# Two transformer blocks on one core: the last layer's expert weights in runs of four rows a partition, and token rows modulated before they are gathered

## The chip, the cores and the metric

The kernel runs on one core of one Trainium2 chip. The core has a matrix engine (TensorE, PE in the profile), a vector engine (VectorE, DVE), a scalar engine (ScalarE, ACT), a GpSimd engine (POOL) and a sync engine (SyncE, SP) that only issues transfers; 16 DMA engines move data between DRAM and the on-chip memory of 128 partitions (SBUF). The metric is the device time of one execution in microseconds; the time of a kernel is the median of its runs.

## What is computed

All in float32, on 512 latent and 256 context tokens of width 1024. A first block of two layers, then a second block of one layer. In each layer of the first block an attention and convolution mixer comes first and then a mixture of experts in which each expert chooses its tokens. The change touches the experts alone:

```python
def modulate(h, shift, scale):
    return h * (1 + scale) + shift

def expert_choice_ffn(h, w_router, w_g, w_u, w_d):
    B, n, D = h.shape
    cap = CAPACITY_FACTOR * n // N_EXPERTS          # 64 latent, 32 context tokens
    logits = jnp.einsum('bnd,de->ben', h, w_router)
    aff = jax.nn.softmax(logits, axis=1)
    gate, idx = lax.top_k(aff, cap)
    xs = h[bi, idx]
    a = jnp.einsum('becd,edf->becf', xs, w_g)
    u = jnp.einsum('becd,edf->becf', xs, w_u)
    y = jnp.einsum('becf,efd->becd', jax.nn.silu(a) * u, w_d)
    return jnp.zeros_like(h).at[bi, idx].add(y * gate[..., None])

# in a layer, after the mixer:
h2 = modulate(rmsnorm(x, g_ffn[l]), sh2, sc2)
x = x + gt2 * expert_choice_ffn(h2, w_router[l], w_e_gate[l], w_e_up[l], w_e_down[l])
```

There are 16 experts a layer, each with three 1024 x 1024 weight matrices (`w_e_gate`, `w_e_up`, `w_e_down`), so that a layer reads 201 MB of expert weights. In the first layer the latent and the context tokens both go through the experts, in the last layer the latent ones alone.

## The kernel before

Stages, in order: mixer of layer 0 for the latent tokens (to about 635 us), the same for the context tokens (to about 873), experts of layer 0 for both (to about 1436), mixer of layer 1 (to about 2053), experts of layer 1 (`experts_local`, to about 2530), second block.

**Weights of the experts.** They pass through a ring of slots, each 128 partitions x 4 rows x 1024 floats (2 MB); a slot holds half of a matrix. `ring_load` (L884) fills one with two transfers of 1 MB on SP's queue; SP issues a load when the slot's last reader on PE is done, so the loads run ahead of their use by the length of the ring (10 slots in layer 0, 9 in layer 1). The source is viewed as `"(k p) f -> p k f"`: partition p gets rows p, 128+p, 256+p, 384+p of the half, and each row is a run of 4 KB on its own. A layer has 96 loads, 192 transfers.

**Token rows.** At the end of a mixer `project` makes the output product, adds it to the rows `xt` (tiles of 128 tokens), and for each tile computes the norm, the router's logits and a row tile `xn`, which is `xt` times the reciprocal norm r:

```python
xo = p.tile([128, D], FP32, name="xn", bufs=2)
self.scale(xo, xt[t], r, t)          # DVE for even tiles, ACT for odd ones (L358, L360)
nc.gpsimd.dma_start(self.dr[f"xn{st.name}{l}"][t * 128:t * 128 + 128], xo)   # L1082
```

There are two buffers for `xn`, and the stores stand in POOL's queue. `choose` then finds the tokens of each expert. `fetch` (L1216, POOL's queue) gathers the 128 chosen rows of two latent experts, or four context ones, from DRAM by an indirect transfer into `xg`. `gather` turns them: eight 128 x 128 transposes on PE (L141) into PSUM, and then eight copies of 128 x 128 to `xT`, each of which also applies the modulation, scale G and shift S being one value a partition there (`affine`: DVE L1127 and ACT L1125 in turn).

**An expert.** `up` (L1239) makes the gate and the up product from `xT` and four slots, `act` the activation `th`, `act_turn` turns it with four (latent) or two (context) transposes and copies it to `hT`, and `down_ps` (L1269) makes the down product from two slots. Matmuls take their operands in order on PE: what stands behind an instruction that waits, waits too. The kernel is built by Tile, a scheduler that puts each engine's instructions in an order at build time.

**The start of the experts of layer 0.** `expert0` fetches, turns and computes the latent part of expert 0 while the context mixer ends; everything else of the stage follows it on PE.

Of the kernel before, what the change touches and what calls it, by code (L numbers as in the profile page):

```python
# [8 lines left out]
FP32 = mybir.dt.float32  # L9
# [3 lines left out]
ACTF = mybir.ActivationFunctionType  # L13
ALU = mybir.AluOpType
# [4 lines left out]
D = 1024  # L19
# [18 lines left out]
class Kernel:  # L38
# [832 lines left out]

    def ring_load(self):

        e, r = divmod(self.nload, 6)
        which, k = divmod(r, 2)
        q, nm = self.cyc[self.nload % self.nring]
        self.nload += 1
        t = self.slots.pop(nm, None)
        if t is None:
            t = q.tile([128, 4, D], FP32, name=nm)  # L880
        src = self.A[("w_e_gate", "w_e_up", "w_e_down")[which]][self.rl, e, k * 512:(k + 1) * 512]
        src = src.rearrange("(k p) f -> p k f", p=128)
        for j in range(2):
            self.nc.sync.dma_start(t[:, 2 * j:2 * j + 2], src[:, 2 * j:2 * j + 2])  # L884
        self.rt[which, e, k] = t
# [149 lines left out]
    def project(self, l, st, wp, p, mg, src, dst, ring, extra):  # L1035

        nc, n, nt, A = self.nc, st.n, st.nt, self.A  # L1040
        gt = p.tile([128, D], FP32, name="gt1")
        md = self.dr[f"mod{l}"]
        nc.sync.dma_start(gt, md[st.s:st.s + 1, 2 * D:3 * D].to_broadcast([128, D]))
        xt = self.load_x(nc.sync, p if dst else self.xs, src, nt)
        wr = p.tile([128, KT, NE], FP32, name="wr")
        nc.sync.dma_start(wr, A["w_router"][l].rearrange("(k p) e -> p k e", p=128))
        ss = self.small.tile([128, 4, 4], FP32, name="ssp")
        G, S = st.aff2
        z = self.small.tile([128, 4, NE], FP32, name="rz", bufs=2)[:, :nt]
        gw = p.tile([128, KT, NE], FP32, name="gw")  # L1050
        sw = self.small.tile([128, NE], FP32, name="sw", bufs=1)

        def router(hs, ws):
            lg = self.s_ps(NE)
            for kt in range(KT):
                nc.tensor.matmul(lg, hs[:, kt], ws[:, kt], start=kt == 0, stop=kt == KT - 1)
            return lg

        def shift():

            sb = p.tile([128, KT, 128], FP32, name="h2", bufs=2)
            for kt in range(KT):
                nc.vector.tensor_copy(sb[:, kt], S[kt].to_broadcast([128, 128]))
                nc.vector.tensor_scalar(gw[:, kt], wr[:, kt], G[:, kt:kt + 1], None, op0=ALU.mult)
            nc.scalar.activation(sw, router(sb, wr), ACTF.Copy)

        def rows(t):

            s1 = self.small.tile([128, 1], FP32, name="s1")
            nc.vector.reduce_sum(s1, ss[:, t], axis=AX.X)  # L1070
            r, _ = self.rsqrt(s1, [128, 1], 1.0 / D, EPS)
            h = p.tile([128, KT, 128], FP32, name="h2", bufs=2)
            for q in range(2):
                tp = self.t_ps(128, 512)
                for i in range(4):
                    self.transpose(tp[:, i * 128:(i + 1) * 128], xt[t][:, (4 * q + i) * 128:(4 * q + i + 1) * 128])
                self.copy(h[:, 4 * q:4 * q + 4], tp.rearrange("p (k c) -> p k c", c=128))
            yield
            nc.vector.scalar_tensor_tensor(z[:, t % 2 * 2 + t // 2 if nt == 4 else t], in0=router(h, gw), scalar=r, in1=sw, op0=ALU.mult, op1=ALU.add)
            xo = p.tile([128, D], FP32, name="xn", bufs=2)  # L1080
            self.scale(xo, xt[t], r, t)
            nc.gpsimd.dma_start(self.dr[f"xn{st.name}{l}"][t * 128:t * 128 + 128], xo)  # L1082
            if not dst:
                self.kept.append(xt[t])
            yield

        tails = []
        for c in range(4):
            cs = slice(c * 256, c * 256 + 256)
            w = self.wblock(wp, A["w_out"][l, :, cs])  # L1090
            if ring and self.nload < len(self.cyc):
                self.ring_load()
            for t in range(nt):
                ts = slice(t * 128, t * 128 + 128)
                ps = self.mm_ps(128, 256)
                self.mm3(ps, mg, w, ts, slice(0, 256))
                y = p.tile([128, 256], FP32, name="py", bufs=2)
                nc.vector.tensor_mul(y, ps, gt[:, cs])
                nc.vector.tensor_add(xt[t][:, cs], xt[t][:, cs], y)
                if dst:  # L1100
                    nc.gpsimd.dma_start(self.dr[dst][ts, cs], xt[t][:, cs])
                nc.scalar.activation(y, xt[t][:, cs], ACTF.Square, accum_out=ss[:, t, c:c + 1])
                if c == 1 and t == 0:
                    shift()
                for g in tails:
                    next(g, None)
                if t % 2:
                    next(extra, None)
                if c == 3:
                    tails.append(rows(t))  # L1110
        for g in [*tails, extra]:
            self.drive(g)
        rm = self.small.tile([128, 2, 4], FP32, name="rmx")
        nc.vector.reduce_max(rm[:, 0, :nt], z, axis=AX.X)
        nc.vector.tensor_tensor(z, z, rm[:, 0, :nt, None].to_broadcast([128, nt, NE]), op=ALU.subtract)
        zf = z.rearrange("p t e -> p (t e)")
        self.exp(p, zf, zf, nt * NE)
        nc.vector.reduce_sum(rm[:, 1, :nt], z, axis=AX.X)
        nc.vector.reciprocal(rm[:, 1, :nt], rm[:, 1, :nt])
        nc.vector.tensor_tensor(z, z, rm[:, 1, :nt, None].to_broadcast([128, nt, NE]), op=ALU.mult)  # L1120
        return z
# [91 lines left out]
    def fetch(self, st, g, p):  # L1213
# [3 lines left out]
            out=st.xg, out_offset=None, in_=self.dr[f"xn{st.name}{st.l}"],  # L1217
            in_offset=bass.IndirectOffsetOnAxis(ap=st.gi[:, g:g + 1], axis=0))

    def gather(self, st, p, p_x, bufs=1):  # L1220

        nc, xg = self.nc, st.xg
        xT = p.tile([128, KT, 128], FP32, name="xT" + st.name, bufs=bufs)
        G, S = st.aff2
        for q in range(2):
            tp = p_x()
            self.pe_run([self.transpose(tp[:, i * 128:(i + 1) * 128], xg[:, (4 * q + i) * 128:(4 * q + i + 1) * 128])
                         for i in range(4)])
            for i in range(4):
                kt = 4 * q + i  # L1230
                self.affine(xT[:, kt], tp[:, i * 128:(i + 1) * 128], G[:, kt:kt + 1], S[kt], i)
        return xT

    def up(self, st, w, e, p_a):
# [20 lines left out]
    def act_turn(self, st, t, p, p_x):  # L1255

        nj = st.w // 128
        tp = p_x()[:, :nj * 128]
        self.pe_run([self.transpose(tp[:, j * 128:(j + 1) * 128], t[:, j * 128:(j + 1) * 128]) for j in range(nj)])
        hT = p.tile([128, 512], FP32, name="hT")[:, :nj * 128]  # L1260
        self.copy(hT, tp)
        return hT
# [158 lines left out]
    def block2(self):  # L1421
# [4 lines left out]
        with ExitStack() as es:  # L1426
# [164 lines left out]
            for t in range(nt):  # L1591
                nc.sync.dma_start(xs[t], self.dr["x2"][t * 128:(t + 1) * 128])
            out_b = project(1, xs, False)
            fill = [(q_gen(Qs, QA + 256, "q_norm_a_2", self.sk[:, 2, 4:8], 1), 5), (gates(Gs[3], GA, 1), 2)], [(out_b, 16)]
            for kv in range(2):
                Vh = [V_[:, t, kv * 64:kv * 64 + 64] for t in range(4)]
                self.section(attend(Qs.pop(0), [(kh[:, kv], kl[:, kv])] * 4, [Vh] * 4, 0, 2 * kv, Gs[2 + kv]),
                             fill[kv], last=kv == 1)
            self.drive(project(0, xs, True))


# [57 lines left out]
```

## Time and profile before

| | before |
|---|---|
| median of 3 runs | 2824.26 us (2823.77 to 2829.33) |
| profiled execution | 2827.67 us, of which the profile's span is 2825.9 us |
| mean granted clock of TensorE | 0.976 |
| PE, DVE, ACT, POOL busy | 93%, 49%, 34%, 4% of the span |
| DMA, mean over the span | 225 GB/s |

A busy share is a mean over stages that have different limits. The page also cuts the span into 40 equal slices, gives busy shares and DMA rates for each, and follows back the chain of work that ended last; windows, waits and timelines of single stretches come from the trace.

### The profile page before, as it was taken

The page shows a single profiled execution, that of the slowest core. Times are in us where ns is not written, and L with a number is a line of the kernel's source. Part 1 is how long each engine was busy: PE and PEld are TensorE (multiplying, and loading weights), DVE is VectorE, ACT ScalarE, POOL GpSimd, SP SyncE. Part 2 cuts the span into 40 slices and gives each one's busy share as a digit, 9 for nine tenths or more (in the row PEclk, how much of TensorE's full clock was granted, in tenths as well). Part 3 has the DMA queues.
Part 4 walks back from the last instruction along what each step waited for, and adds up shares of the span by engine and source line. Part 5 has one row for each costly group of instructions (what it writes and reads, how often), then busy time and mean ns, then how long its engine had stood idle before and what let it go on. Part 6 is the DMA issues. An engine that isn't in the chain of part 4 may idle for free. (4 is left out here: it accounts for less than half of the span.)

```text
span 2825.9 us, 43871 instructions
## 1 busy us (share of the span) xinstructions
PE 2635.3 (93%) x17509; PEld 1811.8 (64%) x17509; DVE 1382.9 (49%) x3755; ACT 962.8 (34%) x1966; POOL 117.6 (4%) x143
## 2 busy tenths in 40 slices
PE   7999999999998999999989999999789888879999
PEld 3788887789995455544437888878733222229878
DVE  4766676459764111111137665764622222238886
ACT  4445455225551000000034454553211000125763
POOL 0100000020001011111000000000000000000000
PEclk9999999999998999999989999999899999999999
DMA  8411211678466999999965212114789999983221
GB/s 291 161 61 60 75 49 59 229 267 299 150 215 223 379 374 384 391 391 387 386 233 171 67 55 75 51 61 131 297 351 409 409 409 409 409 337 87 61 90 60
DMA packets 273839, 635.96 MB, mean 225 GB/s; under 512 B 23924, under 2 KB 148292, under 8 KB 273636
## 3 DMA queue, kind: packets, MB, share of 16 engines
q1 hardware_dynamic: 258868, 595.31, 57.0%
q0 software_dynamic: 13744, 34.68, 4.0%
q8 instruction: 138, 2.26, 0.3%
q10 hardware_dynamic: 1024, 3.18, 0.3%
q14 instruction: 65, 0.53, 0.1%
HBM read 610.75 MB, written 22.35 MB: 224 GB/s over the span
## 5 line engine op out<-in xcount | busy, mean ns | idle before, releaser
L1239 PE MATMUL au<-we,xTlat 128*64 128x512 f32 x1984 | 451.3, 597 | 36.2 <-DMA we<-in_w_e_up_dram 23.4
L1239 PEld LDWEIGHTS au<-we,xTlat 128*64 128x64 f32 x1984 | 156.8, 137 | 320.0 <-issue 207.0
L219 PE MATMUL mm<-hhi,whi 128*128 128x512 f32 (+1 forms) x928 | 338.3, 365 | 0.0
L221 PE MATMUL mm<-hhi,wlo 128*128 128x512 f32 (+1 forms) x928 | 334.4, 360 | 0.0
L220 PE MATMUL mm<-hlo,whi 128*128 128x512 f32 (+1 forms) x928 | 332.6, 358 | 0.0
L199 DVE TENSOR_TENSOR wlo<-wraw,whi 128x1024 fp32r<-128x1024 f32 x234 | 285.6, 1222 | 92.7 <-ACT whi L198 90.8
L198 ACT ACTIVATE whi<-wraw 128x1024 fp32r<-128x1024 f32 x234 | 247.1, 1058 | 170.7 <-PE mm L220 93.6
L1269 PE MATMUL yp<-we,hT 128*32 128x256 f32 (+1 forms) x2016 | 286.6, 493 | 14.5 <-ACT hT L135 7.3
L219 PE MATMUL mm<-whi,hhi 128*128 128x256 f32 x736 | 218.0, 297 | 11.4 <-ACT qr L440 6.3
L1269 PEld LDWEIGHTS yp<-we,hT 128*32 128x32 f32 (+1 forms) x2016 | 112.1, 125 | 166.5 <-issue 109.5
L220 PE MATMUL mm<-wlo,hhi 128*128 128x256 f32 x736 | 214.0, 291 | 1.0 <-DVE wlo L199 1.0
L221 PE MATMUL mm<-whi,hlo 128*128 128x256 f32 x736 | 213.6, 292 | 0.0
L219 PEld LDWEIGHTS mm<-hhi,whi 128*128 128x128 f32 x928 | 175.8, 189 | 26.8 <-issue 4.9
L221 PEld LDWEIGHTS mm<-hhi,wlo 128*128 128x128 f32 x928 | 175.4, 189 | 25.5 <-issue 0.8
L220 PEld LDWEIGHTS mm<-hlo,whi 128*128 128x128 f32 x928 | 175.7, 189 | 24.1 <-issue 1.5
L582 ACT ACTIVATE PT<-tp 128x384 f32<-128x384 f32 (+2 forms) x392 | 142.5, 407 | 113.9 <-PE tp L141 111.6
L554 ACT ACTIVATE P<-S,mx,sc 128x768 f32<-128x768 f32 (+5 forms) x192 | 151.9, 792 | 80.1 <-DVE mx L551 73.2
L1250 ACT ACTIVATE th<-au 128x512 f32<-128x512 f32 (+1 forms) x47 | 24.6, 524 | 447.2 <-PE au L1239 447.2
L219 PEld LDWEIGHTS mm<-whi,hhi 128*128 128x128 f32 x736 | 144.9, 197 | 21.4 <-ACT qr L440 8.3
L1251 DVE SCALAR_TENSOR_TENSOR th<-th,au 128x512 f32<-128x512 f32 (+1 forms) x47 | 28.1, 597 | 247.3 <-ACT th L1250 247.3
L1252 DVE TENSOR_TENSOR th<-th,au 128x512 f32<-128x512 f32 (+1 forms) x47 | 28.1, 597 | 246.1 <-PE au L1239 246.1
L220 PEld LDWEIGHTS mm<-wlo,hhi 128*128 128x128 f32 x736 | 144.8, 197 | 4.3 <-issue 2.6
(319 smaller groups left out, 4560.4 us busy)
## 6 DMA issues: line engine op xcount, KB each, us to landing
we<-in_w_e_gate_dram SPq DMA_DIRECT2D x128, 1024.0 KB, 19.1
we<-in_w_e_up_dram SPq DMA_DIRECT2D x128, 1024.0 KB, 13.8
we<-in_w_e_down_dram SPq DMA_DIRECT2D x128, 1024.0 KB, 18.3
wraw<-in_w_in_dram SPq DMA_DIRECT2D x166, 512.0 KB, 3.8
wada<-in_w_ada_dram SPq DMA_DIRECT2D x96, 512.0 KB, 6.7
wraw<-in_w_branch_dram SPq DMA_DIRECT2D x36, 512.0 KB, 3.5
wraw<-in_w_out_dram SPq DMA_DIRECT2D x32, 512.0 KB, 3.6
xt<-in_x_dram SPq DMA_DIRECT2D x8, 512.0 KB, 8.0
```

Source lines behind the costliest of these rows:

```text
L198: self.nc.scalar.activation(hi, src, ACTF.Copy)
L199: self.nc.vector.tensor_sub(lo, src, hi.bitcast(FP32))
L219: nc.tensor.matmul(ps, lh, rh, start=k == 0, stop=False)
L220: nc.tensor.matmul(ps, lh, rl, start=False, stop=False)
L221: nc.tensor.matmul(ps, ll, rh, start=False, stop=k == n)
L554: nc.scalar.activation(P, S[:, c0:c1], ACTF.Exp, bias=mx[:, 1:2], scale=sc, accum_out=mx[:, 2:3])
L582: self.nc.scalar.activation(PT[:, s0:s0 + j - i, qc:qc + 128], tp[:, i * 128:j * 128].rearrange("p (s c) -> p s c", c=128), ACTF.Copy)
L1239: r = [self.nc.tensor.matmul(ps[j * st.cap:(j + 1) * st.cap], st.xT[:, kt, s0:s0 + st.cap], w[kt // 4][:, kt % 4, j * st.w:(j + 1) * st.w] ...
L1250: nc.scalar.activation(t, a, ACTF.Tanh, scale=0.5)
L1251: nc.vector.scalar_tensor_tensor(t, in0=t, scalar=1.0, in1=a, op0=ALU.add, op1=ALU.mult)
L1252: nc.vector.tensor_tensor(t, t, u, op=ALU.mult)
L1269: r = [self.nc.tensor.matmul(ps[o * st.cap:(o + 1) * st.cap], hT[:, j * 128 + q * st.cap:j * 128 + (q + 1) * st.cap], w[kt // 4][:, kt % 4 ...
```

## The change

Three edits go together.

1. In layer 1 a ring load views its source as `"(p k) f -> p k f"`: partition p gets rows 4p to 4p+3 of the half. The two transfers of a load then take two of these rows each, so a partition reads one run of 8 KB in each, at a distance of 16 KB from the next partition's. Layer 0 keeps its runs of 4 KB.
2. This permutes the rows over which the products of layer 1 contract. So the transposes in `gather` and `act_turn` take, in layer 1, every fourth column (`rows_of`): 8 for each of 8 gathers and 4 for each of 16 experts, 128 in all.
3. The modulation, whose values would be permuted too, moves from `gather` to `project`, in both layers. `row_mod` loads three rows broadcast to all partitions (scale, shift and the norm's gain, 512 KB each, on SP's queue) and makes the factor `gb` on DVE (128 x 1024). Each token tile (4 latent and 2 context ones in layer 0, 4 in layer 1) is scaled by r on ACT, then multiplied by `gb` and added to the shift on POOL, and then stored as before. `gather` now copies plainly, two copies of 128 x 512 (ACT L135 and DVE L137) in place of eight that modulate; there are 8 + 4 gathers in layer 0 and 8 in layer 1.

```diff
@@ ring_load
         src = self.A[("w_e_gate", "w_e_up", "w_e_down")[which]][self.rl, e, k * 512:(k + 1) * 512]
-        src = src.rearrange("(k p) f -> p k f", p=128)
+        src = src.rearrange("(p k) f -> p k f" if self.rl else "(k p) f -> p k f", p=128)
         for j in range(2):
             self.nc.sync.dma_start(t[:, 2 * j:2 * j + 2], src[:, 2 * j:2 * j + 2])
@@ project
         G, S = st.aff2
+        gb, sb2 = [p.tile([128, D], FP32, name=x) for x in ("gb", "sb")]
...
+        def row_mod():
+
+            gf = self.A["g_ffn"]
+            nc.sync.dma_start(gb, md[st.s:st.s + 1, 4 * D:5 * D].to_broadcast([128, D]))
+            nc.sync.dma_start(sb2, md[st.s:st.s + 1, 3 * D:4 * D].to_broadcast([128, D]))
+            g = p.tile([128, D], FP32, name="xn", bufs=2)
+            nc.sync.dma_start(g, gf[l:l + 1].to_broadcast([128, D]))
+            nc.vector.scalar_tensor_tensor(gb, in0=gb, scalar=1.0, in1=g, op0=ALU.add, op1=ALU.mult)
...
             xo = p.tile([128, D], FP32, name="xn", bufs=2)
-            self.scale(xo, xt[t], r, t)
+            nc.scalar.activation(xo, xt[t], ACTF.Copy, scale=r)
+            nc.gpsimd.tensor_mul(xo, xo, gb)
+            nc.gpsimd.tensor_add(xo, xo, sb2)
             nc.gpsimd.dma_start(self.dr[f"xn{st.name}{l}"][t * 128:t * 128 + 128], xo)
...
                 if c == 1 and t == 0:
                     shift()
+                    row_mod()
@@ gather, act_turn
+    def rows_of(self, st, x):
+
+        if st.l:
+            x = x.rearrange("t (c j) -> t j c", c=128)
+            return [x[:, j] for j in range(x.shape[1])]
+        return [x[:, j:j + 128] for j in range(0, x.shape[1], 128)]
...
-        G, S = st.aff2
         for q in range(2):
             tp = p_x()
-            self.pe_run([self.transpose(tp[:, i * 128:(i + 1) * 128], xg[:, (4 * q + i) * 128:(4 * q + i + 1) * 128])
-                         for i in range(4)])
-            for i in range(4):
-                kt = 4 * q + i
-                self.affine(xT[:, kt], tp[:, i * 128:(i + 1) * 128], G[:, kt:kt + 1], S[kt], i)
+            self.pe_run([self.transpose(tp[:, i * 128:(i + 1) * 128], x)
+                         for i, x in enumerate(self.rows_of(st, xg[:, 512 * q:512 * q + 512]))])
+            self.copy(xT[:, 4 * q:4 * q + 4], tp.rearrange("p (k c) -> p k c", c=128))
...
-        self.pe_run([self.transpose(tp[:, j * 128:(j + 1) * 128], t[:, j * 128:(j + 1) * 128]) for j in range(nj)])
+        self.pe_run([self.transpose(tp[:, j * 128:(j + 1) * 128], x) for j, x in enumerate(self.rows_of(st, t))])
```

The scheduler puts the new work into POOL's queue like this. Before, at the end of the context mixer of layer 0 (`Vctx` are the last loads of the context attention, the first `xglat` is the fetch for `expert0`, `c_64` are the mixer's output rows, `xnctx` the row tiles of the context, `x_63` the result of expert 0):

```order
L690 DMA Vctx_6179<-kcs_1120 128x256
L1216 DMA xglat<-xnlat_66,gilat_7458 128x1024
L1101 DMA c_64<-xt 128x256 x8
L1082 DMA xnctx_67<-xn 128x1024 x2
L1284 DMA x_63<-ylat,silat_7459 1024x512
L1216 DMA xglat<-xnlat_66,gilat_7458 128x1024
L1216 DMA xgctx<-xnctx_67,gictx_9484 128x1024
L1216 DMA xglat<-xnlat_66,gilat_7458 128x1024
L1216 DMA xgctx<-xnctx_67,gictx_9484 128x1024
L1284 DMA c_64<-yctx,sictx_9485 1024x256
L1216 DMA xglat<-xnlat_66,gilat_7458 128x1024
```

After, at the same place:

```order
L690 DMA Vctx_6191<-kcs_1114 128x256
L690 DMA Vctx_6194<-kcs_1120 128x256
L1116 DMA c_64<-xt 128x256 x8
L1095 TENSOR_TENSOR xn<-xn,gb 128x1024
L1096 TENSOR_TENSOR xn<-xn,sb 128x1024
L1095 TENSOR_TENSOR xn<-xn,gb 128x1024
L1097 DMA xnctx_67<-xn 128x1024
L1096 TENSOR_TENSOR xn<-xn,sb 128x1024
L1097 DMA xnctx_67<-xn 128x1024
L1232 DMA xglat<-xnlat_66,gilat_7473 128x1024
L1304 DMA x_63<-ylat,silat_7474 1024x512
L1232 DMA xglat<-xnlat_66,gilat_7473 128x1024
```

The first fetch stood ahead of the stores of the context rows; it now stands behind them, behind the four elementwise instructions of the two context tiles and behind their stores.

ACT's queue at the end of the mixer of layer 1, before (`h` are the turned rows for the router, `py` the squares for the norm, `xn` the scaled row tiles):

```order
L358 ACTIVATE xn<-xt,rsq 128x1024
L1102 ACTIVATE py,ssp<-xt 128x256
L135 ACTIVATE h_18469<-tp 128x512
L135 ACTIVATE h_18536<-tp 128x512
L1102 ACTIVATE py,ssp<-xt 128x256
L135 ACTIVATE h_18574<-tp 128x512
L358 ACTIVATE xn<-xt,rsq 128x1024
L1125 ACTIVATE xTlat<-tx,modT_144,G2lat_17873 128x128 x4
```

After, at the same place:

```order
L1094 ACTIVATE xn<-xt,rsq 128x1024
L1117 ACTIVATE py,ssp<-xt 128x256
L135 ACTIVATE h_18426<-tp 128x512
L1117 ACTIVATE py,ssp<-xt 128x256
L1094 ACTIVATE xn<-xt,rsq 128x1024 x2
L135 ACTIVATE h_18495<-tp 128x512
L1117 ACTIVATE py,ssp<-xt 128x256
L135 ACTIVATE h_18535<-tp 128x512
L1094 ACTIVATE xn<-xt,rsq 128x1024
L135 ACTIVATE xTlat<-tx 128x512
```

All four tiles are now scaled on ACT; the third of them (the second of the pair in one row) needs the buffer of the first, and stands ahead of the copies of `h` for the third and fourth tile.

## Rows read from the trace of the kernel before

**Rows 1.** The page: DMA rate in 40 slices, chain by line, a group.

```profile
GB/s 291 161 61 60 75 49 59 229 267 299 150 215 223 379 374 384 391 391 387 386 233 171 67 55 75 51 61 131 297 351 409 409 409 409 409 337 87 61 90 60
...
DMA we<-in_w_e_up_dram 7%; PE mm L219 4%; PE mm L221 3%; PE mm L220 3%; PE au L1239 3%; SPq L884 3%; PE yp L1269 2%; PE tp L141 2%; PE mm L630 1%; DVE wlo L199 1%; PE S L539 1%; PE yp L1383 1%; DVE xt L1387 0%; PE S L540 0%; DVE xq L483 0%
...
L199 DVE TENSOR_TENSOR wlo<-wraw,whi 128x1024 fp32r<-128x1024 f32 x234 | 285.6, 1222 | 92.7 <-ACT whi L198 90.8
```

**Rows 2.** Windows of both expert stages: busy us by engine, PEclk, DMA share, GB/s.

```profile
955.00:1440.00 485.00, 470.65 (x4273) 225.22 (x4268) 70.52 (x140) 37.77 (x78) 53.86 (x37) 1.00 0.98 371
...
2300.00:2400.00 100.00, 80.97 (x346) 27.47 (x344) 23.67 (x41) 9.38 (x18) 1.87 (x2) 0.95 1.03 409
```

**Rows 3.** DMA view, 2150 to 2500 us: packets; one queue (packets, MB, share).

```profile
DMA packets 37153, 143.23 MB, mean 409 GB/s; under 512 B 2219, under 2 KB 2219, under 8 KB 37141
...
q1 hardware_dynamic: 36421, 140.43, 100.5%
```

**Rows 4.** The same view, 1600 to 1900 us: packets and two queues.

```profile
DMA packets 17975, 18.13 MB, mean 60 GB/s; under 512 B 544, under 2 KB 17952, under 8 KB 17952
...
q1 hardware_dynamic: 17952, 17.83, 19.0%
q8 instruction: 14, 0.23, 0.3%
```

**Rows 5.** Line L884, 2064 to 2513 us: transfers, ns, first and last start.

```profile
L884 SPq DMA_DIRECT2D we<-in_w_e_down_dram x60: 367/2351/4417, 2068.1 to 2504.8; - x60
L884 SPq DMA_DIRECT2D we<-in_w_e_up_dram x58: 368/2406/4402, 2064.7 to 2494.1; - x58
L884 SPq DMA_DIRECT2D we<-in_w_e_gate_dram x56: 367/2348/4407, 2075.0 to 2484.3; - x56
```

**Rows 6.** Waits of PE, 2080 to 2512 us: us in total, times, longest.

```profile
PE au L1239 <- DMA we<-in_w_e_up_dram: 22.8, 38, 0.7
PE tx L141 <- ACT xTlat L1125: 15.3, 7, 2.3
```

**Rows 7.** Waits of PE, 955 to 1440 us.

```profile
PE tx L141 <- ACT xTlat L1125: 8.1, 6, 1.3
```

**Rows 8.** Timeline of POOL, 828 to 912 us: start us, us, instruction.

```profile
833.65 1.47 POOL L1216 DMA_INDIRECT xglat<-xnlat,gilat  x1 [192.28 <-PE mm L221]
...
868.31 0.54 POOL L1101 DMA_DIRECT2D c<-xt  x1 [2.63 <-DVE xt L1099]
...
878.10 0.54 POOL L1082 DMA_DIRECT2D xnctx<-xn  x1 [8.58 <-ACT xn L358]
```

**Rows 9.** Timeline of DVE, 866 to 869 us.

```profile
867.93 0.75 DVE L360 TENSOR_SCALAR xn<-xt,rsq 128x1024 f32<-128x1024 f32 x1
```

**Rows 10.** Timeline of PE, 868 to 912 us.

```profile
872.28 1.10 PE L141 MATMUL tp<-ident,xglat 128*128 128x128 f32 x4
...
875.76 14.83 PE L1239 MATMUL mm<-we,xTlat 128*64 128x512 f32 x64
```

**Rows 11.** DMA view, 828 to 912 us: fetches (median us to landing).

```profile
xglat<-xnlat,gilat POOLq DMA_INDIRECT x3, 5.5
```

**Rows 12.** DMA view, 1990 to 2062 us: stores of the rows.

```profile
xnlat<-xn POOLq DMA_DIRECT2D x4, 512.0 KB, 5.4
```

**Rows 13.** DMA view, 955 to 1440 us: fetches.

```profile
xglat<-xnlat,gilat POOLq DMA_INDIRECT x5, 9.3
```

**Rows 14.** Timeline of ACT, 2017 to 2040 us.

```profile
2022.13 1.15 ACT L358 ACTIVATE xn<-xt,rsq 128x1024 f32<-128x1024 f32 x1 [2.54 <-DVE rsq L177]
...
2029.27 0.60 ACT L135 ACTIVATE h<-tp 128x512 f32<-128x512 f32 x1 [4.37 <-PE tp L141]
```

**Rows 15.** Timeline of POOL, 2015 to 2062 us.

```profile
2019.94 0.58 POOL L1082 DMA_DIRECT2D xnlat<-xn  x1 [492.90 <-DVE xn L360]
...
2053.45 1.02 POOL L1216 DMA_INDIRECT xglat<-xnlat,gilat  x1 [15.55 <-DVE ig L1186]
```

**Rows 16.** Tile xglat: instructions that read it (ns min/median/max).

```profile
L141 PE MATMUL tx<-ident,xglat x128: 270/273/477, 908.5 to 2455.8; 128*128 128x128 f32 x128
```

## The prediction

> **What bounds the kernel now.** I read the page first, then windows over the two expert stages, then waits, queues and timelines at the two places where the order of work changes. The page's slices put the DMA rate near 225 GB/s on the whole, but five slices of the last layer's expert stage stand at 409 without a break, and in the chain the largest entry is a wait for the weights of `w_e_up` [rows 1]. The windows say why: from 2300 to 2400 us the DMA engines are busy 1.03 of the time and PE 81%; in the experts of layer 0 the rate is 371 GB/s and PE is busy 470.65 of 485 us [rows 2]. So layer 1's experts run at the pace of the transfers and layer 0's at PE's. The waits agree: in layer 1 PE waits mostly for weights [rows 6], in layer 0 for copies out of PSUM, among which 8.1 us, six times, for `xTlat` [rows 7]. A faster transfer pays in layer 1 alone; a shorter PSUM copy pays in layer 0 alone.
>
> **Term 1, runs of 8 KB.** Line L884 issues 60 + 58 + 56 = 174 transfers from 2064.7 to 2504.8 us [rows 5]. At 1.0486 MB each that is 182.5 MB, and at 409 GB/s 446.1 us. What a packet of 8 KB takes no row shows, so I bound it. The queue's packets there are 36421, of which 2219 are short; taking those as free, 34202 packets of 4 KB share 100.5% of 16 engines x 350 us, 164.6 ns each [rows 3]. In the mixer the same queue moves 17952 - 544 = 17408 packets of 1 KB in 19.0% of 16 x 300 us, 52.4 ns each [rows 4]. A straight line through both has 15 ns a packet and 0.0365 ns a byte, so 8 KB would take 314 ns where two of 4 KB take 329: a rate 4.8% higher, 428.7 GB/s, 425.6 us, **-20.5**. The other end is nothing: the instruction queue's 14 packets of 16.4 KB take 0.3% of the same 4800 us, about 1.03 us each, 63 ns a KB against 40 for the 4-KB packets [rows 4], so longer is not cheaper there. The fit is the nearer row (same queue, same source), but its 1-KB point comes from engines that are mostly idle. I take 421 GB/s, 433.4 us: **-12.7**, between 0 and -20.5.
>
> The Trainium skill ("DMA: Bandwidth & Descriptors", section "Why small descriptors are slow (HBM only)") speaks against the fit: it gives about three cycles a packet at 32 bytes a cycle, 131 cycles for 4 KB and 259 for 8 KB, 1.2% less; by that estimate the term would be -5 and the sum +3. By the rows the fixed part is 15 of 165 ns, four times as much; no run yet shows which holds for 8 KB.
>
> **Term 2, gather without the modulation.** In layer 0 six waits of 8.1 us stand behind the eight small copies [rows 7], 1.35 each. Two copies of 128x512 side by side take 0.60 [rows 14] and leave perhaps 0.35, so **-6**, between 0 and -8. In layer 1 the same waits (15.3 us, seven) [rows 6] lie beside transfers that set the pace: 0.
>
> **Term 3, the first fetch of layer 0.** Before, it was issued at 833.65, ahead of everything; the rows were there when PE turned them at 872.28, and `up` began at 875.76 [rows 8, 10]. Now it stands behind eight `c` stores, four POOL instructions of 128x1024 and two stores. The trace has no elementwise instruction on POOL. The nearest row is DVE's product of two 128x1024 tiles, 1.22 us [rows 1], which I take as the lower end; I take twice that, d = 2.4 us, and four times, 4.9, as the upper end, since nothing in the rows excludes a slower engine. The last `c` store ends at 868.31 + 0.54 [rows 8]; the first tile was scaled from 867.93 on DVE [rows 9], on ACT 1.15 us [rows 14], so POOL starts at about 869.1. The second tile is ready by then or soon after, since its norm no longer waits behind the small copies. Fetch issued at 869.1 + 4d + 2 x 0.54 = 879.8; landing 5.5 us later, the median of fetches around there [rows 11], 885.3; eight transposes of 0.273 [rows 16] and a copy of 0.60, `up` at 888.1: **+12**. With d = 1.22 it is +8, with 4.9 it is +22, and with a landing of 9.3, as it takes in the busy stage [rows 13], +16. All of the stage is queued behind it on PE, and since PE is that stage's bound, nothing gives it back.
>
> The Trainium skill ("GPSIMD Engine Reference", section "3.1 Elementwise — side-by-side cycle accounting") has 4497 ns for an add over 2048 floats, an estimate of 2.25 us for 1024; by it this term would be +11.5.
>
> **Term 4, the rows of layer 1.** The third tile's scale on ACT must wait for the first tile's store, and ahead of two copies of `h`. The first tile is scaled at about 2019.9 + 0.4 (ACT in place of DVE) [rows 15]; products and store on POOL, landing after 5.4 us [rows 12]: 2020.3 + 2d + 5.4 = 2030.5, plus 1.15 [rows 14], so the copy of `h` begins at 2031.7 where it began at 2029.27 [rows 14]: **+2** for logits, choice and first fetch (0 with d = 1.22, +7 with 4.9). The fetch before was at 2053.45 [rows 15]. Eight products and four stores end by 2020.3 + 8d + 2.2, landing 5.4 later, so the stores make the fetch later only from d = 3.2 on; with 4.9 they add another 6.
>
> **At nothing.** The 128 transposes of every fourth column hide under transfers (PE has 19% of the time free there [rows 2]); the first gather doesn't, and pays for them what its plain copies save. The nine row loads (4.6 MB) lie in mixers that move about 50 to 75 GB/s in most slices [rows 1]. The four loads of `hhi` and `hlo` that now stand behind one POOL product at the end of the first mixer cost d at the most if their use has no slack.
>
> **Sum.** -12.7 - 6 + 12 + 2 = -4.7 us. Against the profiled execution, 2827.67, that is 2823.0; this lay 3.4 above the median of the runs, so 2819.5.
>
> **Rivals.**
> - *Row rate and a quick POOL.* 428.7 GB/s and d = 1.22: -20.5 - 6 + 8 = -18.5, 2805.8. For it speaks the straight line, and a POOL that is as quick as DVE; against it that the line rests on two points.
> - *The run brings nothing.* An 8-KB run moved as two packets of 4 KB, or at the same ns a byte, leaves 446.1 us: -6 + 12 + 2 = +8, 2832.3, slower. The gain of term 1 decides the sign: below 8 us (416 GB/s) the late fetch outweighs it. The instruction queue's packets speak for it. The rule on three cycles that I named lies on this side, at +3.
> - *A slow POOL.* With d = 4.9, +22 and +13 against -12.7 and -6: +16, 2840.4. Each us of d costs 4 us in layer 0 and 2 in layer 1, so the sum turns positive at d = 3.2. Against it: it is four times DVE's row.
> - *Transposes that bind.* PE works 81% of an expert's 30.8 us (12.58 MB at 409), 24.9 us [rows 2]. An expert has eight of the changed transposes (its half of a gather, and its own four); at four times 0.273 us [rows 16] they add 6.6, 31.5 us an expert, above the transfers' 29.9. Over 14.5 experts that is +10 instead of -12.7, and +6.6 for the first gather: +25, 2849. Below 3.3 times they stay hidden. No row of before reads floats four apart into PE, neither for it nor against.
>
> The Trainium skill ("SBUF — State Buffer", section "Specifications (TRN2)") speaks for this last one: lines of 16 bytes, and a read needs two hits a line for full bandwidth; a stride of four floats hits each line once. No row here shows it.
>
> **Chances.** Forecast 0.44, row rate 0.16, nothing gained 0.23, slow POOL 0.13, binding transposes 0.04. About 0.2% (5.6 us) can be told from no change. The forecast's own range is -14 to +3 us (2810 to 2827): of its 0.44, 0.25 falls on faster, 0.16 on the same, 0.03 on slower. Row rate: all faster. Nothing gained: 0.07 same, 0.16 slower. Slow POOL: 0.01, 0.02 and 0.10. Transposes: slower. Sums 0.42, 0.25, 0.33. The range runs from just under the row rate's time to just under the slow POOL's: 2804 to 2838.
>
> **What would show it.** In windows of the last expert stage the rate should read about 421 in place of 409, and the last ring load be issued some 10 us sooner after the first; at 409 or at 428 the second or the first rival holds. POOL's products should read 1.2 to 3 us. The first `up` of layer 0 should begin some 12 us later after the context mixer, with PE idle ahead of it for the fetch. In layer 0 PE's waits for `xTlat` should fall to 2 us. The changed transposes should read within three times 0.273 us. The prediction is wrong if the rate stays, if POOL takes over 3.2 us, or if an idle PE makes the granted clock fall in layer 0 by more than the few us that I left out.

## The result and the profile after

| | before | changed |
|---|---|---|
| median of 5 runs | 2826.30 us (2823.77 to 2829.92) | 2844.99 us (2838.93 to 2852.24) |
| profiled execution (span) | 2827.67 (2825.9) | 2850.19 (2848.4) |
| mean granted clock of TensorE | 0.976 | 0.972 |

The change made the kernel slower: ratio 1.0065, 95% interval 1.0049 to 1.0082. That is 18.7 us on the medians and 22.5 between the two profiled executions, on which the rest is told. The five runs of the changed kernel span 13 us and the profiled one lies 5 above their median, so a single stretch of it is good to some us only.

The windows over the expert stages come first (columns as in [rows 2]):

```profile
960.00:1440.00 480.00, 474.42 (x4316) 221.93 (x4316) 62.66 (x111) 29.07 (x54) 51.86 (x36) 1.00 1.02 389
...
2300.00:2400.00 100.00, 85.62 (x374) 28.42 (x370) 22.06 (x34) 8.61 (x14) 0.94 (x1) 1.00 1.01 421
```

The last stage does run faster: 421 GB/s for 409, and PE 86% busy for 81%. The queue view of 2150 to 2500 us, as [rows 3], tells why:

```profile
DMA packets 20558, 147.17 MB, mean 420 GB/s; under 512 B 2285, under 2 KB 2285, under 8 KB 2925
...
q1 hardware_dynamic: 19825, 144.35, 99.2%
```

Packets of 8 KB are 20558 - 2925 = 17633, and they share 99.2% of 16 x 350 us: 315 ns each, where the line through two points had 314. The rate rose by 2.8% only, and not by the line's 4.8%, because the engines' summed share fell from 1.03 to 1.01: packets overlap less.

Where the time is lost is read from a few instructions that both kernels have. All times are starts, in us; the last column is how much the lateness changed over the stretch:

| instruction | before | changed | late by | in this stretch |
|---|---|---|---|---|
| last `c` store (end of layer 0's context mixer, but for the rows) | 868.31 | 881.81 | 13.5 | +13.5 |
| first `up` of expert 0 | 875.76 | 909.26 | 33.5 | +20.0 |
| last scatter of layer 0 | 1437.06 | 1459.20 | 22.1 | -11.4 |
| first fetch of layer 1 | 2053.45 | 2086.05 | 32.6 | +10.5 |
| first store of the result of layer 1's experts | 2531.59 | 2552.81 | 21.2 | -11.4 |

The rows of the last three instructions, first before and then changed (the others stand in [rows 8, 10, 15] and below):

```profile
1437.06 1.55 POOL L1284 DMA_INDIRECT c<-yctx,sictx  x1 [1.79 <-DVE yctx L1282]
2531.59 0.58 POOL L1439 DMA_DIRECT2D x<-xt  x1 [136.96 <-DVE xt L1387]
```

```profile
1459.20 1.55 POOL L1304 DMA_INDIRECT c<-yctx,sictx  x1 [1.79 <-DVE yctx L1302]
2086.05 1.02 POOL L1232 DMA_INDIRECT xglat<-xnlat,gilat  x1 [15.55 <-DVE ig L1202]
2552.81 0.58 POOL L1459 DMA_DIRECT2D x<-xt  x1 [133.41 <-DVE xt L1407]
```

Two stages gain 11.4 us each, and the ends of the mixers with the first fetch lose 44. POOL's timeline at the first fetch, the answer to [rows 8]:

```profile
881.81 0.54 POOL L1116 DMA_DIRECT2D c<-xt  x1 [1.74 <-DVE rsq L173]
884.90 2.34 POOL L1095 TENSOR_TENSOR xn<-xn,gb 128x1024 f32<-128x1024 f32 x1 [2.55 <-ACT xn L1094]
887.32 2.34 POOL L1096 TENSOR_TENSOR xn<-xn,sb 128x1024 f32<-128x1024 f32 x1
891.58 2.37 POOL L1095 TENSOR_TENSOR xn<-xn,gb 128x1024 f32<-128x1024 f32 x1 [1.92 <-ACT xn L1094]
893.90 0.56 POOL L1097 DMA_DIRECT2D xnctx<-xn  x1
894.48 2.35 POOL L1096 TENSOR_TENSOR xn<-xn,sb 128x1024 f32<-128x1024 f32 x1
897.12 0.57 POOL L1097 DMA_DIRECT2D xnctx<-xn  x1 [0.30 <-POOL xn L1096]
898.00 1.03 POOL L1232 DMA_INDIRECT xglat<-xnlat,gilat  x1 [0.30 <-issue]
```

And the timeline of PE there, as [rows 10]:

```profile
907.38 1.94 PE L141 MATMUL tp<-ident,xglat 128*128 128x128 f32 x8 [21.11 <-DMA xglat<-xnlat,gilat]
909.26 3.12 PE L1259 MATMUL mm<-we,xTlat 128*64 128x512 f32 x8
```

The fetch is issued at 898.00, behind four products, and PE sits idle for 21.11 us until its rows land. The landing is the last number of its row in the DMA view of 870 to 912 us:

```profile
xglat<-xnlat,gilat POOLq DMA_INDIRECT x1, 9.2
```

9.2 us. Between the last `c` store and the first product lie 3.1 us, and 1.92 before the third, `<-ACT xn`: the scale on ACT came late. ACT's timeline tells what it waited for:

```profile
883.68 1.14 ACT L1094 ACTIVATE xn<-xt,rsq 128x1024 f32<-128x1024 f32 x1
890.36 1.15 ACT L1094 ACTIVATE xn<-xt,rsq 128x1024 f32<-128x1024 f32 x1 [5.54 <-DVE rsq L177]
```

5.54 us for `rsq`, the reciprocal norm of the second tile, a chain of tiny instructions on DVE. The groups of POOL's products and DVE's line of that chain hold the answer. First POOL's groups (line, operation, count, busy us, mean ns):

```profile
L1096 POOL TENSOR_TENSOR xn<-xn,sb 128x1024 f32<-128x1024 f32 x10 | 24.6, 2462 | 0.5
L1095 POOL TENSOR_TENSOR xn<-xn,gb 128x1024 f32<-128x1024 f32 x10 | 23.7, 2373 | 513.7 <-ACT xn L1094 513.7
```

POOL takes 2.4 us for an instruction, just the d that was assumed. Next the timeline of POOL in layer 1:

```profile
2043.25 2.38 POOL L1096 TENSOR_TENSOR xn<-xn,sb 128x1024 f32<-128x1024 f32 x1
...
2048.37 2.37 POOL L1095 TENSOR_TENSOR xn<-xn,gb 128x1024 f32<-128x1024 f32 x1 [1.81 <-ACT xn L1094]
2050.82 2.34 POOL L1096 TENSOR_TENSOR xn<-xn,sb 128x1024 f32<-128x1024 f32 x1
```

and DVE's over the same time:

```profile
2043.41 2.23 DVE L173 SCALAR_TENSOR_TENSOR rsq<-rsq 128x1 f32<-128x1 f32 x1
2045.68 0.16 DVE L177 SCALAR_TENSOR_TENSOR rsq<-rsq 128x1 f32<-128x1 f32 x1
...
2046.57 0.21 DVE L173 SCALAR_TENSOR_TENSOR rsq<-rsq 128x1 f32<-128x1 f32 x1
...
2048.11 0.22 DVE L173 SCALAR_TENSOR_TENSOR rsq<-rsq 128x1 f32<-128x1 f32 x1
...
2048.56 2.20 DVE L173 SCALAR_TENSOR_TENSOR rsq<-rsq 128x1 f32<-128x1 f32 x1
2050.79 0.16 DVE L177 SCALAR_TENSOR_TENSOR rsq<-rsq 128x1 f32<-128x1 f32 x1
2050.99 2.19 DVE L173 SCALAR_TENSOR_TENSOR rsq<-rsq 128x1 f32<-128x1 f32 x1
```

DVE's instruction on L173, 128 elements in all, usually takes 0.22 us. Three of those shown take 2.2: they start at 2043.41, 2048.56 and 2050.99, while a POOL product runs, and end at 2045.64, 2050.76 and 2053.18, within 0.02 us of that product's end (2045.63, 2050.74, 2053.16). Over the whole kernel (count, ns min/median/max, first and last start), before and changed:

```profile
L173 DVE SCALAR_TENSOR_TENSOR rsq<-rsq x51: 209/219/221, 22.8 to 2539.0; 128x1 f32<-128x1 f32 x51
```

```profile
L173 DVE SCALAR_TENSOR_TENSOR rsq<-rsq x51: 207/220/2414, 23.1 to 2559.8; 128x1 f32<-128x1 f32 x51
```

Such an instruction stands until POOL's product is done, and what follows it in DVE's queue stands with it. Not every instruction of DVE does: beside the product that starts at 633.22, two with one input of 128x1 (633.71 and 633.77) take their usual 0.14 us.

### The profile page after: what moved, and what is told of

It is laid out like the page before. It is cut to its first block, busy times and chain, and to the rows that moved or that the text cites. A ratio compares the mean times of both kernels' runs of the same rounds, so it can differ in the third digit from the quotient of the medians.

```text
span 2848.4 us, 43803 instructions
## 1 busy us (share of the span) xinstructions
PE 2642.3 (93%) x17509; PEld 1815.0 (64%) x17509; DVE 1399.3 (49%) x3690; ACT 946.1 (33%) x1908; POOL 165.8 (6%) x163
## 3 DMA queue, kind: packets, MB, share of 16 engines
q10 hardware_dynamic: 1024, 3.18, 0.3%
## 4 chain that ended last, share of the span: by engine, by line
PE 28%; DMA 16%; issue 14%; DVE 6%; ACT 2%; POOL 2%; ACTq 0%; POOLq 0%; SPq 0%; DVEq 0%
PE mm L219 6%; PE mm L221 5%; PE mm L220 5%; DMA we<-in_w_e_down_dram 5%; DMA we<-in_w_e_up_dram 5%; DMA we<-in_w_e_gate_dram 4%; PE au L1259 3%; PE tp L141 3%; PE mm L630 2%; PE yp L1289 1%; PE S L539 1%; DVE wlo L199 1%; PE S L540 1%; POOL c L1304 1%; POOL x L1304 1%
## 5 line engine op out<-in xcount | busy, mean ns | idle before, releaser
L199 DVE TENSOR_TENSOR wlo<-wraw,whi 128x1024 fp32r<-128x1024 f32 x234 | 287.7, 1231 | 92.9 <-ACT whi L198 90.8
```

Source lines behind the costliest of these rows:

```text
L199: self.nc.vector.tensor_sub(lo, src, hi.bitcast(FP32))
```

## The experiments

The theory: **a lock**. While GpSimd runs an instruction that reads tiles in SBUF, an instruction of VectorE with two such inputs waits until it is done. The rival: **the queue**. All of the loss is what stands behind the products on POOL's own queue (fetch, stores, buffers). Each run was timed against before on the same chip. Unless told otherwise the edits are against the changed kernel.

**1. The layout undone.**

```diff
-        src = src.rearrange("(p k) f -> p k f" if self.rl else "(k p) f -> p k f", p=128)
+        src = src.rearrange("(k p) f -> p k f", p=128)
...
-        if st.l:
-            x = x.rearrange("t (c j) -> t j c", c=128)
-            return [x[:, j] for j in range(x.shape[1])]
```

> The changed kernel with the layout of layer 1 undone (runs of 4 KB, plain transposes), modulated rows kept. Theory of the lock (VectorE's instructions wait while GpSimd runs a product of two tiles) and its rival (all losses come from what stands behind the products in GpSimd's queue) both expect the transfers at 409 GB/s again and the 11 us that the last expert stage gained to be gone: about 2856 us. If the transposes of every fourth column cost something there, less than that.

Measured: 2855.00 us, ratio to before 1.0103 (1.0082 to 1.0123). From the first fetch of layer 1 to the first store of the result it takes 477.5 us, against 466.8 with the layout and 478.1 before. So the layout is worth 11 us, and it is not where the loss is. The run also prices the strided transposes; these are PE's groups from 2095 to 2500 us in it:

```profile
L141 PE MATMUL tx<-ident,th 128*128 128x128 f32 x56 | 9.8, 280 | 5.6 <-ACT xTlat L135 4.5 <-DVE th L1269 0.8 <-DVE xTlat L137 0.4
L141 PE MATMUL tx<-ident,xglat 128*128 128x128 f32 x56 | 8.3, 273 | 0.0
```

and in the changed kernel:

```profile
L141 PE MATMUL tx<-ident,th 128*128 128x128 f32 x56 | 10.7, 295 | 5.6 <-ACT xTlat L135 4.5 <-DVE th L1272 0.8 <-DVE xTlat L137 0.3
L141 PE MATMUL tx<-ident,xglat 128*128 128x128 f32 x56 | 8.8, 283 | 0.0
```

10 to 15 ns on 280 for a stride of four floats.

**2. The products on VectorE.**

```diff
-            nc.gpsimd.tensor_mul(xo, xo, gb)
-            nc.gpsimd.tensor_add(xo, xo, sb2)
+            nc.vector.tensor_mul(xo, xo, gb)
+            nc.vector.tensor_add(xo, xo, sb2)
```

> The changed kernel with the product and the sum of the row tiles on VectorE in place of GpSimd; the first fetch of layer 0 keeps its place behind the stores of the context rows. The lock expects no instruction of VectorE above its usual time, the ends of all three mixers back to within 3 us a piece, the first fetch some 8 us late: about 2818 us. The rival expects the wait for the fetch to halve and the rest to stay: about 2832 us.

Measured: 2834.14 us, 1.0025 (1.0014 to 1.0036), between the two expectations. No instance of L173 takes over 0.222 us. The last `c` store is at 874.93, 6.6 us late and not 13.5; the fetch of layer 1 follows the last scatter after 622.7 us (626.9 in the changed kernel, 616.4 before); the first `up` is at 897.26, 22.3 behind the `c` store, 27.5 in the changed kernel, 7.4 before. So each of the three losses is smaller here than in the changed kernel's trace, and none is gone: the fetch is still behind the stores, and the ends of the mixers are late by more than the 3 us a piece that I allowed. I put that down to DVE's own twenty instructions; no run parts them from the scaling on ACT and the row loads. The first of the three is no evidence by itself: in experiment 1, whose layer 0 is the changed kernel's with POOL's products, the last `c` store is at 874.10, 5.8 us late.

**3. The layout alone.** The kernel before, with edit 1 and 2 of the change; the modulation stays in `gather`, its scale and shift for layer 1 loaded in the permuted order (three loads of 4 KB, one instruction on DVE).

```diff
+        if l:
+            gp = self.const.tile([128, 3, 2, 4], FP32, name="gp")
+            for i, v in enumerate((md[st.s:st.s + 1, 4 * D:5 * D], md[st.s:st.s + 1, 3 * D:4 * D], A["g_ffn"][l:l + 1])):
+                nc.sync.dma_start(gp[:, i], v.rearrange("o (q c j) -> c (o q) j", q=2, j=4))
+            nc.vector.scalar_tensor_tensor(gp[:, 0], in0=gp[:, 0], scalar=1.0, in1=gp[:, 2], op0=ALU.add, op1=ALU.mult)
...
-        G, S = st.aff2
+        G, S = st.affp if st.l else st.aff2
```

> The kernel before with the runs of 8 KB and the transposes of every fourth column in layer 1, and the modulation left in the gather, with scale and shift loaded in the permuted order: no row is modulated in the mixer, GpSimd does no arithmetic. Both theories expect the 11 us of the transfers and no loss: about 2815 us. If the transposes of every fourth column or the small loads cost, above 2820.

Measured: 2816.05 us, 0.9964 (0.9948 to 0.9981): faster than before, as both theories expect. The permutation needed neither the modulated rows nor POOL.

**4. Idle products on POOL.** The kernel before, with for each tile:

```diff
             nc.gpsimd.dma_start(self.dr[f"xn{st.name}{l}"][t * 128:t * 128 + 128], xo)
+            jk = p.tile([128, D], FP32, name="jk")
+            nc.gpsimd.tensor_mul(jk, xo, gt)
+            nc.gpsimd.tensor_add(jk, jk, gt)
```

> The kernel before with a product and a sum of 128x1024 on GpSimd for each row tile, behind the tile's store, into a tile that nobody reads; the first fetch of layer 0 keeps its early place. The lock expects VectorE's small instructions of 0.2 us to show 2 us beside them, and the ends of the mixers late by about 10 us after layer 0's latent part and 9 us in layer 1: 2842 to 2848 us. The rival expects no row late beyond its own buffer: below 2830 us.

Measured: 2856.44 us, 1.0100 (1.0078 to 1.0122), with the first fetch early (847.59) and the stores ahead of the products. Nothing waits for what POOL makes, and yet the last `c` store is at 880.65, 12.3 us late, and the fetch of layer 1 follows the last scatter after 631.6 us, where it was 616.4 before. DVE's line L173 in it (count, ns min/median/max, first and last start):

```profile
L173 DVE SCALAR_TENSOR_TENSOR rsq<-rsq x51: 206/220/2635, 22.5 to 2568.3; 128x1 f32<-128x1 f32 x51
```

The expectation of the lock was even too small by 8 us. Transfers (`hhi`, `xk`, `Vctx`) stand behind the products in POOL's queue here too; experiment 8 has them behind other work of POOL and loses nothing, so the queue alone cannot do this.

**5. The first fetch early.** The changed kernel, the rows of layer 0's latent tokens gathered into a pool of their own:

```diff
+        if ahead and not lat:
+            self.x0 = self.tc.alloc_tile_pool(name="x0", bufs=1, side="right", reuse_waits="tile")
+            self.rpools.append(self.x0)
...
+        if st is self.lat and not st.l:
+            p = self.x0
         st.xg = p.tile([128, D], FP32, name="xg" + st.name, bufs=1)
```

> The changed kernel, with the tile of the gathered latent rows of layer 0 in a space of its own, so that the first fetch stands in GpSimd's queue ahead of the stores and products of the context rows; all else kept. The lock alone moved the end of the context mixer by 12 us in the run with idle products, and the changed kernel's first product of the experts was another 20 us late. If that 20 is the place in the queue, the first up product begins at 886 to 890 us and the time is about 2825 us; if it is the lock too, it begins after 900 and the time stays above 2838.

Measured: 2836.26 us, 1.0032 (1.0021 to 1.0042); the first `up` at 893.51, 15.7 us sooner than in the changed kernel and 15.4 behind its last `c` store (27.5 there, 7.4 before). That is between the two expectations, 12 of the 20 us, and what is left comes from another order: PE turns the rows of a second fetch ahead of the first `up` here, and that fetch stands behind a product. PE's timeline of this run:

```profile
882.70 0.63 PE L141 MATMUL tp<-ident,xglat 128*128 128x128 f32 x4
891.64 1.94 PE L141 MATMUL tx<-ident,xglat 128*128 128x128 f32 x8 [8.30 <-DMA xglat<-xnlat,gilat]
893.51 2.83 PE L1264 MATMUL mm<-we,xTlat 128*64 128x512 f32 x6
```

Experiment 4, with its fetch early, PE's order as before and products of the same length on POOL, has its first `up` (887.67) 7.0 us behind the `c` store. So the loss at the fetch is one of place: behind the products, whose length and late start are part of it.

**6. Both: early fetch, products on VectorE.** Edits of 2 and 5 together.

> The same early fetch with the product and the sum of the rows on VectorE. Of the 34 us by which the run on VectorE was above the sum of the two gains, the wait for the fetch is seen as 11; the rest is the arithmetic itself on VectorE. Expected 2823 us; if the wait was the most of it, about 2815; if the place does not count, 2834.

Measured: 2827.99 us, 1.0001 (0.9991 to 1.0010): no difference from before. By stretches: last scatter of layer 0 at 1437.77 against 1437.06, so the 12.1 us that the plain gather gains there are taken back by 4.5 at the end of the mixer and 8.4 at the first `up`, which is 15.8 behind the `c` store; from there to the first fetch of layer 1 625.7 us against 616.4, 9.3 more, which eats most of what the layout gives. Against experiment 2 the early fetch is worth 7 us, each taken against its own runs of before (0.2 above them here, 7.2 there), not the 11 that were seen as its wait; so the time is 5 us above the expectation.

**7. One run of 16 KB.** The layout alone (3), a load as one transfer of four rows a partition:

```diff
-        for j in range(2):
-            self.nc.sync.dma_start(t[:, 2 * j:2 * j + 2], src[:, 2 * j:2 * j + 2])
+        c = 4 if self.rl else 2
+        for j in range(0, 4, c):
+            self.nc.sync.dma_start(t[:, j:j + c], src[:, j:j + c])
```

> The kernel with the layout alone, and each load of layer 1 as one transfer of 2 MB with one run of 16 KB a partition. A straight line in the packet times (314 ns for 8 KB measured as worked out) gives 613 ns for 16 KB against two of 314, 2.6% more rate: about 431 GB/s and 2806 us. If the engines' overlap falls as it did from 4 to 8 KB, 425 and 2811. If a load that frees one slot at a time in place of two halves makes the ring wait, 2816 or more.

Measured: 2809.86 us, 0.9944 (0.9928 to 0.9961), the fastest of all, 0.56% under before. Its queue view from 2150 to 2450 us:

```profile
DMA packets 9334, 128.22 MB, mean 427 GB/s; under 512 B 1043, under 2 KB 1043, under 8 KB 1662
...
q1 hardware_dynamic: 8623, 125.51, 98.4%
```

9334 - 1662 = 7672 packets of 16 KB in 98.4% of 16 x 300 us: 616 ns each, 613 by the line; the rate is 427 GB/s. Rate and time lie between the first two expectations.

**8. POOL busy, but only writing.** The kernel before, with, in place of the idle products:

```diff
+            nc.gpsimd.tensor_copy(jk[:, 0:1], xo[:, 0:1])
+            for _ in range(4):
+                nc.gpsimd.memset(jk, 0.0)
```

> The kernel before with, for each row tile, four fills of 128x1024 on GpSimd into a tile that nobody reads, behind a copy of one column: GpSimd busy as long as with the idle products, but writing alone. If VectorE waits for GpSimd whenever that works, the ends of the mixers are late as with the idle products, about 2850 us. If it waits for the reading of two tiles alone (the lock on a shared read port), its small instructions with two inputs keep their 0.2 us and the time is 2827 to 2832.

Measured: 2829.51 us, 1.0010 (1.0000 to 1.0019), with POOL busy 38.2 us in 40 fills, nearly the 47.5 of the idle products. DVE's line L173 in it:

```profile
L173 DVE SCALAR_TENSOR_TENSOR rsq<-rsq x51: 210/219/221, 22.5 to 2540.3; 128x1 f32<-128x1 f32 x51
```

The longest is 0.22 us, where it was 2.64 beside the products. A busy POOL cost 1.7 us on the medians here; one that reads two tiles cost 29 in experiment 4. Not all of DVE goes free, though; DVE's timeline from 615 to 660 us:

```profile
638.77 1.40 DVE L186 TENSOR_SCALAR h<-h 128x64 f32<-128x64 f32 x1
...
640.20 1.40 DVE L187 TENSOR_SCALAR h<-h 128x64 f32<-128x64 f32 x1
```

These two have one input and took 1.40 us in place of 0.2, each beside a fill.

## Why the prediction was wrong

**Term 1, runs of 8 KB (-12.7): right.** -11.4 in the profiled executions, 9 to 11 on the medians of experiments 1 and 3. The packet's time was on the line of [rows 3, 4] to 1 ns, and at 16 KB to 3. The instruction queue's packets, which spoke for the rival that gains nothing, were no guide, and the rule on three cycles (section "Why small descriptors are slow (HBM only)" of the Trainium skill's "DMA: Bandwidth & Descriptors") was not borne out: with 0.0365 ns a byte taken off, 15 to 18 ns a packet are left over at each of the four sizes measured. What the line did not hold is the overlap: rate and packet time are not each other's inverse.

**Term 2, plain gather (-6): right in kind, mis-sized.** -11.4 from the first `up` to the last scatter. From the first latent `up` of expert 1 to the last scatter, experiments 1 and 2 and the changed kernel all take 504.9 us, before and experiments 3 and 4 all 514.7, so 9.8 of it is the gathers inside the stage. PE's waits for `xTlat` fell from 8.1 [rows 7] to 1.3 us; I had left 2 of them. That is 6.8 of the 9.8; I counted nothing for the context's gathers, and no run shows whether the other 3 are theirs.

**Term 3, the first fetch (+12): mis-sized, +20.** Place and duration were right, and POOL's d was 2.4 us as taken. What made it 20 is in the timelines above. POOL's first product started 3.1 us after the last `c` store and not 0.8; the second tile was scaled at 890.36, and not "by then or soon after", since its norm waited on DVE behind POOL's products; and the fetch landed after 9.2 us (median 5.5 in [rows 11]), about as in the busy stage ([rows 13]).

**Term 4 (+2) and "at nothing": this is the step that failed.** I followed the products of POOL through POOL's queue, the stores and the buffers of `xn`, and took DVE to run beside them. It does not. Layer 1's rows cost 10.5 us and not 2. The 13.5 us by the end of layer 0's context mixer are in no term at all: the list of what costs nothing names the row loads and four loads behind a POOL product there, and not DVE. Experiment 4 is 12.3 us late there with products that nobody waits for, and 29 us above before in all; experiment 8 shows that a POOL that is nearly as busy but only writes is on time there and costs 1.7 us in all. The Trainium skill ("SBUF — State Buffer", section "Who interferes with whom") states it: the two engines share a port pair, and a DVE instruction with two inputs in SBUF contends with a GpSimd instruction that reads SBUF, not with one that only writes, while the two-port forms with one input contend with both. Experiments 4 and 8 agree with the first half; the one-input instructions of 1.40 us beside a fill fit the second, but the trace doesn't tell their form.

How much the lock takes differs from one execution to the next. From the 14th of the 16 `x` stores, the last ahead of POOL's first product, to the last `c` store, before and experiments 3, 7 and 8 take 249.4 to 251.7 us. The changed kernel and experiments 4 and 5 take 263.2 to 264.0, but experiment 1, with the same products, 257.1, which is within the 255.6 to 257.5 of experiments 2 and 6 with the products on VectorE. From the last scatter to the first fetch of layer 1 the three groups stand apart: 612.3 to 618.8, 626.9 to 631.6 and 622.7 to 625.7. And 2.0 of the 13.5 us were there before POOL's first product (618.63 for that `x` store, 616.65 before).

How the lock makes the rest out of stalls is seen in part. From 618 to 665 us DVE's instructions are stretched by some 2 us at a time, among them the split of the weights (L199). PE waits 5.0 us for it from 600 to 700 us, 0.5 before, and SP's next weight loads wait for it too; ACT then sits 8 us twice for weights, 3.3 at most before. The clock is lower there too, a sign that the prediction named. Windows of 640 to 660 and 660 to 700 us, columns as in [rows 2], before:

```profile
640.00:660.00 20.00, 16.41 (x134) 15.74 (x133) 16.93 (x55) 11.13 (x22) 1.37 (x3) 1.00 1.07 370
660.00:700.00 40.00, 39.31 (x323) 37.70 (x322) 38.84 (x119) 21.38 (x42) 0.00 (x0) 1.00 0.87 308
```

and changed:

```profile
640.00:660.00 20.00, 15.92 (x110) 15.52 (x110) 17.24 (x45) 6.49 (x7) 10.01 (x7) 0.86 0.64 208
660.00:700.00 40.00, 35.69 (x263) 33.88 (x264) 33.63 (x104) 19.70 (x42) 3.84 (x4) 0.91 0.86 295
```

A granted clock of 0.86 and 0.91 in place of 1.00, between the levels of 1.2 and 2.4 GHz, is 20 x 0.14 + 40 x 0.09, or 6 us at the most (an estimate from these rows). From 640 to 700 us it is 0.90 in experiment 4 too, 0.96 in experiment 1 and 1.00 in experiment 8. What the row loads on SP's queue cost no run parts from this.

**Rivals.** The sign was that of the rivals on the slow side, and the time near the slow POOL's, for a reason that none of them had: POOL was not slow. The transposes cost 10 to 15 ns each in place of the 620 or so that would have bound ((29.9 - 24.9) / 8 us); of the 16-byte lines that the Trainium skill names, no more than that shows in them.

## What to carry to other kernels

Before an elementwise step goes to GpSimd, look at what VectorE does in the same microseconds: a product of two tiles there stops VectorE's two-input instructions for its whole length, and a chain of 0.2-us instructions that decides when the next stage starts becomes a chain of 2-us ones. Price a moved step on every engine that it can stop and not only on the queue that it joins. And take a bundle apart: of the edits here the layout alone is worth 11 us, with 16-KB runs 16 to 18, and the modulated rows, with the plain gather's gain already in, cost 29 (2845.0 against 2816.1; experiment 1, which has them without the layout, is 28 above before).

## What the runs showed of the hardware that was not expected

- Packets of 1, 4, 8 and 16 KB took 52, 165, 315 and 616 ns: 0.0365 ns a byte and 15 to 18 ns more. The rates of a saturated queue were 409, 420 and 427 GB/s for runs of 4, 8 and 16 KB.
- A GpSimd product of 128x1024 floats took 2.37 us, a fill of the same tile 0.96 us; VectorE takes 1.22 for the same product (experiment 2).
- Beside a fill, the two-input instruction of VectorE on L173 keeps its 0.22 us, and some one-input ones of 0.2 us take 1.4. Beside a product it is the other way with the smallest: 2.4 us for L173, 0.14 as usual for two one-input ones of 128x1.
